# A trunk layer on one Trainium2 core: LayerNorm's sum of squares in a PSUM bank, and one more two-product pair in the up projection

## The chip, the core and the metric

The kernel runs on one core of a Trainium2 chip. The metric is the device time of one execution in microseconds (us); lower is better. The core has five engines with queues of their own, which run beside each other and meet through semaphores: TensorE (PE, the matrix products, with weight loads shown apart as PEld), VectorE (DVE), ScalarE (ACT), GpSimd (POOL) and SyncE (SP, which issues most transfers). Products land in PSUM, which has eight banks of 128 x 512 numbers; everything else lies in SBUF.

## The reference

One decoder layer over 512 tokens of 1024 channels in float32, cut here to what the change touches:

```python
u = rmsnorm(h);  proj = u @ w_in                       # GLU | q | k | v | r | low | gates A, B
c = causal_dwconv(a * sigmoid(g), width 31)            # branch A
c = silu(layernorm(c));  y_conv = c @ w_conv_out       # mean and variance over the channels
y_gla = gla(q, k, v, ...) * silu(r) @ w_gla_out        # branch B, four heads
h = h + (sigmoid(gate_a) * y_conv + sigmoid(gate_b) * y_gla) @ w_o
u2 = rmsnorm(h)
z = causal_dwconv(u2 @ w_ffn_up, width 3)              # 1024 -> 2 x 2816
h = h + (silu(z[:, :2816]) * z[:, 2816:]) @ w_ffn_down
out = rmsnorm(h)
```

## The kernel before, in words

**Products in three parts.** Each float32 operand is split into a high part (`whi` for weights) and the rest (`wlo`); a product is then three: high x low, low x high, high x high (`mm3`, lines 516 to 522). These three lines are nearly all of TensorE's work. A weight tile is 128 rows of 1024 numbers (512 KB); SyncE fetches it into `raw` (four buffers), and `split_weight` (lines 396 to 445) makes its parts in four `whi` and four `wlo` buffers: ScalarE copies the high part, VectorE subtracts it from `raw` for the low part (line 443, or 409 for tiles of other kinds). For the names in `ADDED` (lines 47 and 48) VectorE isn't used: ScalarE writes -`raw` into `wlo` (line 440) and a transfer issued from GpSimd's queue adds the weight tile to it from HBM (line 441). The high part is the same. `LOOK = 2` (line 45): parts are made two tiles ahead.

**Order.** The weights are used in one list, `order`, from line 242 on; each call of `weight` takes the next. A scheduler turns the program into one queue for each engine and picks the buffers, so a change in one stage can move the places of neighbouring instructions in a queue.

**The up projection.** Its 44 tiles of 128 channels come as 22 pairs (i, 22 + i): the value half and the gate half of one block. There are three groups of blocks (`GROUPS`, line 34). The first is ((0, 2), (1, 3), (4, 6), (5, 7)); in each inner pair the first block has the role "first" and the other "second", after the place that it takes in the down projection that follows the group. A plain tile (`col_tile`, line 524) is 8 x 3 products of 512 columns, 24 in all. Two tiles can be had for fewer multiplications (`two_tiles`, line 1313): the tokens are halved, and seven products of weight sums with token sums take the place of eight. That is four weight operands x1, x3, x2, x4 (two, two, two and one steps), each step 4 x 3 products of 256 columns, 84 in all. x3 and x4 are weight sums that GpSimd makes (`two_sums`, lines 377 to 392, line 380 in the profile): three adds of 128 x 512 at x1 and one at x3. VectorE combines the seven results (line 1323). The token sums are made once, by VectorE and ScalarE, in the first group (`ffn_sums`, lines 1276 to 1289 in the profile).

**The plan of a group** (`up_plan`, lines 187 to 231) is a list of steps. In the first group, blocks 0 and 2 are done ahead of it; then blocks 1, 3 and 4 are plain; then come two units. A unit is one two-product pair with a plain block threaded through its parts: pair 6 with block 5, pair 7 with block 8 (a block of the next group). After each block its width-3 convolution runs: ScalarE scales (line 1690), VectorE adds two taps (line 1693), and then the gating and splits for the down projection (`first_gated`, `first_of_pair`, `second_of_pair`, lines 1716 to 1740). The loop at line 1845 carries the plan out; `third` (set when a pair is done) is an order that the next "second" step keeps: it is placed behind the pair's last tap and the third weight sum.

**LayerNorm of branch A** runs beside the merge stage, as a chain of small steps that `fill` (line 496) deals out among the tiles. The mean lies in an "ax" bank of PSUM (there are three). For each of eight channel blocks `ln_center` (line 1002) subtracts the mean (line 1003), squares (line 1005, ScalarE) and adds the square to `stat["sq"]` (line 1009, VectorE). The sum and each square are "btmp" tiles in SBUF, of which there are two. `token_sums` then multiplies the sum with ones.

Of the kernel before, what the change touches and what calls it, by code (L numbers as in the profile page):

```python
# [15 lines left out]
ALU = mybir.AluOpType  # L16
# [5 lines left out]
KT = D // P  # L22
# [6 lines left out]
FT = FF // P  # L29
# [69 lines left out]
def trunk_layer(ctx: ExitStack, tc: tile.TileContext, a: dict, out: bass.AP):  # L99
    nc = tc.nc  # L100
# [33 lines left out]
    def btmp():  # L134
        return tp.tile([P, T], F32, tag="btmp", name=nm("btmp"), bufs=2)
# [50 lines left out]

    def up_plan(gi):


        pairs = GROUPS[gi]  # L190
        whole = range(KT)

        def halves(*cuts):
            return [range(a, b) for a, b in zip((0, *cuts), (*cuts, KT))]

        def unit(q, f, kind):

            a, b = f, FT + f
            x1, x3, x2, x4 = (("part", q, part) for part in ("x1", "x3", "x2", "x4"))
            a1, a2 = (("tile", a, ks) for ks in halves(4))  # L200
            if kind == "opens":
                b1, b2, b3 = (("tile", b, ks) for ks in halves(4, 6))
                seq = [a1, x1, a2, x3, b1, x2, b2, x4, ("second", q), b3]
            elif kind == "closes":
                a1, a2, a3 = (("tile", a, ks) for ks in halves(3, 6))
                seq = [x1, a1, x3, a2, x2, a3, x4, ("second", q), ("tile", b, whole)]
            else:
                a1, a2 = (("tile", a, ks) for ks in halves(5))
                b1, b2 = (("tile", b, ks) for ks in halves(4))
                seq = [x1, a1, x3, a2, x2, b1, x4, ("second", q), b2]  # L210
            return seq + [("first", f)]

        firsts = [p for p, _ in pairs[1:]]
        if gi + 1 < len(GROUPS):
            firsts.append(GROUPS[gi + 1][0][0])
        plan = []
        n = 0
        if gi == 0:
            (p, q), (f, _) = pairs[1:3]
            for i, role in ((p, "first"), (q, "second"), (f, "first")):  # L220
                plan += [("tile", i, whole), ("tile", FT + i, whole), (role, i)]
            n = 2
        while n < len(firsts):
            last = n + 1 == len(firsts) and gi + 1 < len(GROUPS)
            kind = "closes" if last else "opens" if n == 0 else ""
            plan += unit(pairs[n][1], firsts[n], kind)
            n += 1
        if n < len(pairs):
            q = pairs[n][1]
            plan += [("tile", q, whole), ("tile", FT + q, whole), ("second", q)]  # L230
        return plan

    def up_order(plan):
# [767 lines left out]

    def ln_center(k):
        nc.vector.tensor_tensor(conv[k], stat["mean"], conv[k], ALU.add)
        sq = btmp()
        nc.scalar.activation(sq, conv[k], AF.Square)
        if k == 0:
            stat["sq"] = sq
        else:
            nc.vector.tensor_tensor(stat["sq"], stat["sq"], sq, ALU.add)

    def ln_var():
        v = small(NT, "mean")
# [805 lines left out]
    for gi, pairs in enumerate(GROUPS):  # L1818
        acts = []
        if gi == 0:  # L1820

            ws = [weight("w_up", j, 0) for i in pairs[0] for j in (i, FT + i)]
            accs = [mm_bank() for _ in ws]
            for j, lo in [(j, lo) for lo in (0, H) for j in range(3)]:
                late = {(1, 0): (KT - 1, 2), (2, 0): (MID, 3)}.get((j, lo))
                at = {late[0]: lambda t=late[1]: to_channels(normed[t], u2, t)} if late else {}
                col_tile(ws[j], acts2, accs[j], lo, lo + H, at)
            col_tile(ws[3], acts2, accs[3])
            p, q = pairs[0]
# [12 lines left out]
            some_sums()  # L1842
        else:
            found = first_of_pair(w)
        for what, i, *rest in up_plan(gi):
            if what == "tile":
                if 0 in rest[0]:
                    banks[i] = (weight("w_up", i), mm_bank())
                wt, acc = banks[i]
                col_tile(wt, acts2, acc, ks=rest[0])  # L1850
                if KT - 1 in rest[0] and i < FT:
                    values[i] = value(i, acc)
            if what == "part":
                if rest[0] == "x1":
                    units[i] = two_tiles("w_up", i, FT + i, lambda: up_acts, ax_bank)
                done = next(units[i])
                if done:
                    values[i] = value(i, done[0])
                    banks[FT + i] = (None, done[1])
                    third = [taps_at[0], third_ahead()]  # L1860
            if what == "first":
                w = first_gated(i, values.pop(i), banks.pop(FT + i)[1])
                if any(i in pair for pair in pairs):
                    found = first_of_pair(w)
            if what == "second":
                with ExitStack() as order_of:
                    for ins in third:
                        if ins:
                            order_of.enter_context(tc.issue_after(ins.ins))
                    acts.append(second_of_pair(i, values.pop(i), banks.pop(FT + i)[1], w, found))  # L1870
                third = []
            if what in ("first", "second"):
                some_sums()
        if gi < len(GROUPS) - 1:
            seven("w_down", pairs, acts, lambda t, n, c: None)
        else:
            gain3 = load_gain("final_g")
            seven("w_down", pairs, acts, last_complete, last_at, True)
# [90 lines left out]
```

## Time and profile before

| | us |
|---|---|
| median of three runs | 827.72 |
| the three runs | 827.73, 827.72, 824.37 |
| the profiled execution | 824.33 |
| its span, first to last instruction | 822.3 |
| TensorE busy in the span | 808.5 |
| VectorE, ScalarE, GpSimd busy | 707.6, 482.7, 182.4 |
| the first group of the up projection, TensorE | 474.0 to 573.2 |
| LayerNorm's eight centerings, VectorE | 314.9 to 324.1 |

The granted TensorE clock is 0.998 of full speed over the span. A row of a timeline begins with the start and the duration in us and names engine, line, operation, output <- inputs, partitions x elements; what stands in brackets is the engine's idle time before it and who ended it. A row of the groups ends with the busy time in us and the mean duration in ns of one. Matmul durations overlap, so the pace of TensorE is read from the starts.

### The profile page before, as it was taken

What the parts mean: (1) busy time and instruction counts of PE and PEld (TensorE: products, weight loads), DVE (VectorE), ACT (ScalarE), POOL (GpSimd) and SP (SyncE); (2) the same over time, 40 slices, a digit from 0 to 9 for tenths busy, and PEclk for the clock granted to TensorE, in tenths of its full rate; (3) what the DMA queues carried; (4) which work ended last, traced back from release to release, by engine and by line L of the source; (5) the groups of instructions that cost most, each with busy time, mean ns of one, the idle gap of its engine ahead of it and who ended that gap; (6) DMA issues with size and microseconds to landing.
All of it is one profiled execution on the core that took longest, in us unless ns stands there. A gap on an engine that the chain in (4) does not pass through costs nothing.

```text
span 822.3 us, 11449 instructions
## 1 busy us (share of the span) xinstructions
PE 808.5 (98%) x4227; PEld 695.2 (85%) x4227; DVE 707.6 (86%) x1125; ACT 482.7 (59%) x726; POOL 182.4 (22%) x164
## 2 busy tenths in 40 slices
PE   9999999999999999999999999999999999999996
PEld 8888887888887798889988898898889988899885
DVE  6879999999999877595788889979975999789895
ACT  6667788477646574484445546556435663466554
POOL 2016423121203232222001000230133311622012
PEclk9999999999999999999999999999999999999999
DMA  8487886864900433333447623146632447234662
GB/s 325 154 194 166 200 210 168 193 153 103 205 27 26 129 103 103 110 112 111 156 103 219 194 74 103 50 156 163 138 137 83 146 129 166 103 103 173 161 128 102
DMA packets 36759, 114.64 MB, mean 139 GB/s; under 512 B 3720, under 2 KB 8976, under 8 KB 36704
## 3 DMA queue, kind: packets, MB, share of 16 engines
q1 hardware_dynamic: 28912, 86.39, 30.5%
q0 software_dynamic: 7776, 27.53, 19.7%
q8 instruction: 33, 0.54, 0.3%
q14 instruction: 22, 0.18, 0.1%
q10 hardware_dynamic: 16, 0.00, 0.0%
HBM read 111.81 MB, written 2.10 MB: 139 GB/s over the span
## 4 chain that ended last, share of the span: by engine, by line
PE 89%; DVE 4%; issue 3%; DMA 2%; ACT 1%; POOL 0%; POOLq 0%; ACTq 0%; DVEq 0%; SPq 0%
PE mm L520 21%; PE mm L521 21%; PE mm L522 21%; PE cv L520 4%; PE cv L521 4%; PE cv L522 4%; PE ax L522 2%; PE ax L521 2%; PE ax L520 2%; PE mm L734 2%; DVE wlo L409 2%; DMA wlo<-in_w_qk_dram 1%; PE cv L734 1%; PE ax L1201 1%; PE ax L1183 1%
## 5 line engine op out<-in xcount | busy, mean ns | idle before, releaser
L520 PE MATMUL mm<-uh,wlo 128*128 128x512 f32 (+1 forms) x524 | 192.7, 368 | 0.9 <-DMA wlo<-in_w_qk_dram 0.9
L521 PE MATMUL mm<-ul,whi 128*128 128x512 f32 (+1 forms) x524 | 190.7, 364 | 0.0
L522 PE MATMUL mm<-uh,whi 128*128 128x512 f32 (+1 forms) x524 | 190.4, 363 | 0.0
L409 DVE TENSOR_TENSOR wlo<-raw,whi 128x1024 fp32r<-128x1024 f32 x82 | 95.6, 1173 | 30.1 <-ACT whi L408 26.3
L380 POOL TENSOR_TENSOR raw<-raw,raw 128x512 f32<-128x512 f32 x39 | 61.6, 1580 | 240.0 <-DVE wlo L409 122.2
L520 PEld LDWEIGHTS mm<-uh,wlo 128*128 128x128 f32 x524 | 99.0, 189 | 16.7 <-ACT btmp L913 1.3
L522 PEld LDWEIGHTS mm<-uh,whi 128*128 128x128 f32 x524 | 98.8, 189 | 15.7
L521 PEld LDWEIGHTS mm<-ul,whi 128*128 128x128 f32 x524 | 99.0, 189 | 14.7
L408 ACT CAST whi<-raw 128x1024 fp32r<-128x1024 f32 x82 | 79.0, 965 | 38.1 <-PE mm L522 28.5
L438 ACT CAST whi<-raw 128x1024 fp32r<-128x1024 f32 x80 | 83.3, 1046 | 29.1 <-PE mm L522 12.9
L443 DVE TENSOR_TENSOR wlo<-raw,whi 128x1024 fp32r<-128x1024 f32 x50 | 65.9, 1324 | 7.3 <-ACT whi L438 7.1
L408 ACT CAST whi<-kept 128x1024 fp32r<-128x1024 f32 (+1 forms) x40 | 40.1, 1006 | 40.7 <-DVE kept L356 19.2
L880 DVE SCALAR_TENSOR_TENSOR aside<-cv,pp,aside 128x255 f32<-128x255 f32 (+6 forms) x112 | 52.9, 472 | 0.8 <-ACT cv L871 0.8
L409 DVE TENSOR_TENSOR wlo<-kept,whi 128x1024 fp32r<-128x1024 f32 (+1 forms) x40 | 48.2, 1206 | 5.4 <-ACT whi L408 5.2
L880 DVE SCALAR_TENSOR_TENSOR c<-aside,btmp,c 128x249 f32<-128x249 f32 (+14 forms) x103 | 51.4, 509 | 0.7 <-ACT c L876 0.7
L440 ACT ACTIVATE wlo<-raw 128x1024 fp32r<-128x1024 f32 x30 | 31.7, 1058 | 33.8 <-PE mm L520 30.6
L880 DVE SCALAR_TENSOR_TENSOR c<-cv,pp,c 128x255 f32<-128x255 f32 (+14 forms) x103 | 48.6, 472 | 2.9 <-ACT c L876 2.9
L1693 DVE SCALAR_TENSOR_TENSOR tmp<-mm,pp,tmp 128x511 f32<-128x511 f32 (+1 forms) x48 | 35.6, 743 | 4.0 <-ACT tmp L1690 3.9
L1473 DVE TENSOR_TENSOR hres<-hres,mm 128x512 f32<-128x512 f32 (+1 forms) x39 | 25.8, 669 | 3.1 <-PE mm L522 1.7
L1693 DVE SCALAR_TENSOR_TENSOR tmp<-tmp,pp,tmp 128x511 f32<-128x511 f32 (+1 forms) x32 | 27.8, 888 | 0.3
L520 PE MATMUL cv<-uh,wlo 128*128 128x512 f32 (+1 forms) x80 | 27.4, 342 | 0.7 <-DVE tmp L1323 0.7
L1690 ACT ACTIVATE tmp<-mm,pp 128x512 f32<-128x512 f32 x24 | 18.6, 777 | 14.8 <-PE mm L522 14.6
(464 smaller groups left out, 2064.9 us busy)
## 6 DMA issues: line engine op xcount, KB each, us to landing
raw<-in_w_up_dram SPq DMA_DIRECT2D x44, 512.0 KB, 3.6
raw<-in_w_glu_dram SPq DMA_DIRECT2D x16, 512.0 KB, 6.2
raw<-in_w_down_dram SPq DMA_DIRECT2D x15, 512.0 KB, 3.4
wlo<-in_w_glu_dram POOLq DMA_DIRECT2D x12, 512.0 KB, 7.3
kept<-in_w_down_dram POOLq DMA_DIRECT2D x10, 512.0 KB, 5.5
raw<-in_w_v_dram SPq DMA_DIRECT2D x8, 512.0 KB, 6.1
raw<-in_w_qk_dram SPq DMA_DIRECT2D x8, 512.0 KB, 6.6
wlo<-in_w_qk_dram POOLq DMA_DIRECT2D x8, 512.0 KB, 7.1
```

The costliest lines, as they stand in the source:

```text
L380: work = nc.gpsimd.tensor_tensor(out, x, y, ALU.add)
L408: nc.scalar.copy(hi, raw)
L409: two_low[:] = [nc.vector.tensor_tensor(lo, raw, hi.bitcast(F32), ALU.subtract)]
L438: nc.scalar.copy(hi, raw)
L440: pace[0] = nc.scalar.mul(lo, raw, -1.0)
L443: pace[0] = nc.vector.tensor_tensor(lo, raw, hi.bitcast(F32), ALU.subtract)
L520: nc.tensor.matmul(acc, ll, rh, start=first, stop=False, **kw)
L521: nc.tensor.matmul(acc, lh, rl, start=False, stop=False, **kw)
L522: nc.tensor.matmul(acc, lh, rh, start=False, stop=last, **kw)
L880: nc.vector.scalar_tensor_tensor(out[:, j:], x[:, : half_t - j], w, out[:, j:], ALU.mult, ALU.add)
L1473: done = nc.vector.tensor_tensor(hres[t, n][:, c], hres[t, n][:, c], acc[:, c], op)
L1693: nc.vector.scalar_tensor_tensor(z[:, s:], acc[:, : T - s], w[j], z[:, s:], ALU.mult, ALU.add)
```

## The change

It does three things.

- `ln_center`: the sum of squares starts in an "ax" bank (ScalarE writes the first square there), VectorE adds the next six squares onto it in PSUM, and the last add writes the total into a "btmp" tile. One btmp tile less is held over the chain.
- The plans of the groups are written out in `PLANS`. The second and third group's come out as before. In the first group, block 4 (tiles 4 and 26) becomes a two-product pair: blocks 1 and 3 plain, then pair 4 and pair 6 in sequence with block 5 threaded through both, then pair 7 with block 8 as before. The first group has three two-product pairs where it had two. A "first" block can now come from a pair, so the order in `third` is kept there too.
- The low parts of the four plain tiles of blocks 1 and 3 (tiles 1, 23, 3, 25) are put into `ADDED`.

```diff
+PLANS = (
+    (("plain", 1, 3), ("both", 4, 6, 5), ("closes", 7, 8)),
+    (("opens", 10, 9), ("", 11, 20), ("closes", 21, 12)),
+    (("opens", 14, 13), ("", 15, 16), ("", 18, 17), ("plain", 19)),
+)
...
+ADDED |= {("w_up", m) for m in (1, FT + 1, 3, FT + 3)}
...
+        def both(p, q, f):
+
+            x1, x3, x2, x4 = parts(p)
+            y1, y3, y2, y4 = parts(q)
+            (a1, a2), (b1, b2) = cut(f, 4), cut(FT + f, 4)
+            return [x1, a1, x3, a2, x2, x4, role(p), y1, b1, y3, b2, y2, y4, role(q), role(f)]
...
-        sq = btmp()
+        sq = btmp() if k else ax_bank()
         nc.scalar.activation(sq, conv[k], AF.Square)
         if k == 0:
             stat["sq"] = sq
         else:
-            nc.vector.tensor_tensor(stat["sq"], stat["sq"], sq, ALU.add)
+            total = stat["sq"] if k < KT - 1 else btmp()
+            nc.vector.tensor_tensor(total, stat["sq"], sq, ALU.add)
+            stat["sq"] = total
...
             if what == "first":
-                w = first_gated(i, values.pop(i), banks.pop(FT + i)[1])
-                if any(i in pair for pair in pairs):
-                    found = first_of_pair(w)
+                with ExitStack() as order_of:
+                    for ins in third:
+                        if ins:
+                            order_of.enter_context(tc.issue_after(ins.ins))
+                    w = first_gated(i, values.pop(i), banks.pop(FT + i)[1])
+                    if any(i in pair for pair in pairs):
+                        found = first_of_pair(w)
+                third = []
```

In `cut(f, 4)`, `a1` is the first half of block 5's value tile (four of its eight k steps) and `a2` the rest; `b1` and `b2` are the same of its gate tile.

More of the change, by code (lines that the diff above doesn't have):

```diff
@@ L191, in up_plan, with parts, cut @@
         whole = range(KT)
[L193 to L200, printed above, removed]
+        def parts(q):
+            return [("part", q, part) for part in ("x1", "x3", "x2", "x4")]
+        def cut(m, *at):
+            return [("tile", m, range(a, b)) for a, b in zip((0, *at), (*at, KT))]
@@ L201, in unit, with turns, one @@
+        def turns(m, role):
+            return [("tile", m, whole), ("tile", FT + m, whole), (role, m)]
+        def one(q, f, kind):
+            x1, x3, x2, x4 = parts(q)
             if kind == "opens":
-                b1, b2, b3 = (("tile", b, ks) for ks in halves(4, 6))
-                seq = [a1, x1, a2, x3, b1, x2, b2, x4, ("second", q), b3]
+                (a1, a2), (b1, b2, b3) = cut(f, 4), cut(FT + f, 4, 6)
+                seq = [a1, x1, a2, x3, b1, x2, b2, x4, role(q), b3]
             elif kind == "closes":
-                a1, a2, a3 = (("tile", a, ks) for ks in halves(3, 6))
@@ L206, in unit @@
-                seq = [x1, a1, x3, a2, x2, a3, x4, ("second", q), ("tile", b, whole)]
-            else:
[L208 to L215, printed above, removed]
-        plan = []
-        n = 0
@@ L218, in up_plan @@
[L218 to L230, printed above, removed]
+                a1, a2, a3 = cut(f, 3, 6)
@@ new lines, in one @@
+                seq = [x1, a1, x3, a2, x2, a3, x4, role(q), ("tile", FT + f, whole)]
+            else:
+                (a1, a2), (b1, b2) = cut(f, 5), cut(FT + f, 4)
+                seq = [x1, a1, x3, a2, x2, b1, x4, role(q), b2]
+            return seq + [role(f)]
+        def both(p, q, f):
[3 more added lines that the diff above has]
+            return [x1, a1, x3, a2, x2, x4, role(p), y1, b1, y3, b2, y2, y4, role(q), role(f)]
@@ L231, in up_plan, with role @@
+        seconds = {q for _, q in pairs}
+        def role(i):
+            return ("second" if i in seconds else "first", i)
+        plan = []
+        for kind, *units in PLANS[gi]:
+            if kind == "plain":
+                for i in units:
+                    plan += turns(i, role(i)[0])
+            elif kind == "both":
+                plan += both(*units)
+            else:
+                plan += one(*units, kind)
         return plan
```

## The prediction

> **What bounds the kernel now.** I read the page first (span, busy time, chain that ended last), then who waited for whom on TensorE, then the timeline where the two edits lie.
>
> ```profile
> span 822.3 us, 11449 instructions
> ## 1 busy us (share of the span) xinstructions
> PE 808.5 (98%) x4227; PEld 695.2 (85%) x4227; DVE 707.6 (86%) x1125; ACT 482.7 (59%) x726; POOL 182.4 (22%) x164
> ...
> PE 89%; DVE 4%; issue 3%; DMA 2%; ACT 1%; POOL 0%; POOLq 0%; ACTq 0%; DVEq 0%; SPq 0%
> ```
>
> ```profile
> PE mm L520 <- DVE r L1523: 1.9, 1, 1.9
> PE mm L521 <- DVE wlo L409: 1.5, 1, 1.5
> PE mm L640 <- DVE ones L613: 1.1, 1, 1.1
> PE mm L520 <- DMA wlo<-in_w_qk_dram: 0.9, 1, 0.9
> PE cv L520 <- DVE tmp L1323: 0.7, 1, 0.7
> ```
>
> TensorE is busy 98% of the span and is 89% of the chain. Its named waits are single events of 0.7 to 1.9 us. So an edit is worth two things only: the matmul time that it removes, and the part of such a wait that it ends. Work taken off or put on the other engines is worth nothing unless TensorE comes to wait. One wait in the list is touched: the last, 0.7 us on a combine of line 1323.
>
> **Part 1, the extra two-product pair (tiles 4 and 26).** Two plain tiles are 2 x 8 x 3 = 48 products of 512 columns; a pair is 7 steps x 4 x 3 = 84 products of 256 columns. TensorE's timeline gives both rates: first product of the plain tile 26, first of the pair of 6, first after that pair's x1 part.
>
> ```profile
> 525.74 0.39 PE L520 MATMUL cv<-uh,wlo 128*128 128x512 f32 x1
> ...
> 531.18 0.28 PE L520 MATMUL mm<-uh,wlo 128*128 128x256 f32 x1
> ...
> 534.05 0.40 PE L520 MATMUL mm<-uh,wlo 128*128 128x512 f32 x1
> ```
>
> The plain tile takes 531.18 - 525.74 = 5.44 us for 24 products (227 ns each, though each shows 0.39: they overlap). The x1 part takes 2.87 us for 24 (120 ns each). The pair therefore costs 84 x 0.1196 = 10.04 us and replaces 10.88: **-0.84 us**. The column count alone (21504 against 24576) would give -1.36; a short product costs a little over half of a long one. The products lie on the engine that bounds, so nothing hides or eats the gain unless an operand is late.
>
> **Part 2, the sum of squares in PSUM.** VectorE's, GpSimd's and TensorE's timelines around the 0.7 us wait:
>
> ```profile
> 326.03 0.69 DVE L1402 TENSOR_TENSOR h<-mm,h 128x512 f32<-128x512 f32 x1
> 326.64 1.39 DVE L1009 TENSOR_TENSOR btmp<-btmp,btmp 128x512 f32<-128x512 f32 x1
> 327.94 2.31 DVE L409 TENSOR_TENSOR wlo<-raw,whi 128x1024 fp32r<-128x1024 f32 x1
> 330.18 1.77 DVE L1009 TENSOR_TENSOR btmp<-btmp,btmp 128x512 f32<-128x512 f32 x1
> 331.87 0.41 DVE L1323 TENSOR_TENSOR tmp<-tmp,cv 128x256 f32<-128x256 f32 x1
> ```
>
> ```profile
> 326.17 3.00 POOL L380 TENSOR_TENSOR raw<-raw,raw 128x512 f32<-128x512 f32 x2 [13.56 <-ACT btmp L1005]
> 329.13 2.27 POOL L380 TENSOR_TENSOR raw<-raw 128x512 f32<-128x512 f32 x1
> ```
>
> ```profile
> 331.22 0.39 PE L522 MATMUL mm<-oa,whi 128*128 128x512 f32 x1
> 332.34 0.39 PE L520 MATMUL cv<-uh,wlo 128*128 128x256 f32 x1 [0.73 <-DVE tmp L1323]
> ```
>
> ```profile
> L1003 DVE TENSOR_TENSOR c<-ax,c 128x512 f32<-128x512 f32 x8 | 5.1, 684 | 0.0
> ```
>
> While GpSimd adds from 326.17 to 331.4, the VectorE adds that read two SBUF tiles stretch: the sums of squares to 1.39 and 1.77 us, the low part to 2.31. The add with a PSUM input at 326.03 keeps 0.69, and so do the centerings (684 ns). The combine that frees TensorE's bank is behind them in VectorE's queue and begins at 331.87. TensorE should go on 0.23 us after 331.22, at 331.45; it does at 332.34: 0.89 us, and 0.1 more while its pipe refills. In the changed program's queue order the combine stands ahead of the last but one sum of squares and of that low part. The adds and centerings before it all have a PSUM input. From 326.03 I count: one h add 0.6, one centering 0.6, then the combine, ready when its product ends near 327.3. It begins near 327.8, over 3 us ahead of its need. No row shows VectorE *writing* PSUM. Its bounds are the 0.68 of L1003 and the 1.77 of the slowest old sum; I take 0.69, the nearest rows being those with a PSUM input. At 1.77 for each of the five sums ahead of it the combine would begin 5 x 1.08 = 5.4 us later, at 333.2 instead of 331.87 now, and the part would cost 1.3. The last sum goes to SBUF and is needed long after. **-0.95 us**, bounds -1.0 and +1.3.
>
> The Trainium skill, "SBUF — State Buffer", section "Who interferes with whom", says that a VectorE instruction with two SBUF inputs contends with a GpSimd instruction that reads SBUF, and that one with at most one SBUF input, outside the two-port modes, does not. The trace agrees: 1.39 and 1.77 against 0.69 in one stretch. By that rule the new sums can't reach the 1.77, and the part gives -0.95; without it the end of +1.3 has only the distance of the rows against it.
>
> The bank that the sum holds is one of three "ax" banks, and the mean holds another. No other product goes to an ax bank between the mean and the token sums, so nothing queues behind it. The freed btmp buffer lets ScalarE square earlier; ScalarE isn't near the path there.
>
> **Part 3, low parts of tiles 1, 23, 3 and 25 by adding transfers.** VectorE loses four operations of 1.22 us; ScalarE gains four, GpSimd's queue four transfers of 512 KB, all ahead of its adds for pair 4.
>
> ```profile
> L440 ACT ACTIVATE wlo<-raw x30: 1041/1060/1089, 38.5 to 216.9; 128x1024 fp32r<-128x1024 f32 x30
> ```
>
> ```profile
> DMA to landing us min/median/max: 5.3/7.2/10.3
> ```
>
> ```profile
> DMA to landing us min/median/max: 8.5/9.0/9.5
> ```
>
> ```profile
> 498.74 0.78 ACT L1690 ACTIVATE tmp<-mm,pp 128x512 f32<-128x512 f32 x1
> ```
>
> ```profile
> 509.42 0.39 PE L520 MATMUL mm<-uh,wlo 128*128 128x512 f32 x1
> ```
>
> The first landing row is of all 30 such transfers, the second of two issued 1.9 us apart (at 205.3 and 207.2). The tight one is tile 3. In the changed ScalarE queue its -raw copy stands right behind the operation at 498.74, which waits for the product ending there and is delayed to about 499.3 by two earlier copies. So the copy ends near 501.1 and the transfer leaves then. Tile 25's leaves 2 us later. As the first of a close pair I give it 7.2 to 8.5 us: landing at 508.3 to 509.6. Tile 3's first product, which reads the low part, is due at 509.42. **+0.1 us**, bounds 0 and 501.1 + 10.3 - 509.42 = 2.0. The others have room. Tile 1 is due two tiles earlier, 509.42 - 2 x 5.44 = 498.5. Its buffer's last reader ends one tile and two halves before that (5.4 + 2 x 2.9), at 487.2; the copy ends at 488.3 and the transfer lands by 496.8. Tiles 23 and 25 have 2 us or more. ScalarE's four copies fall in idle stretches (it is busy 4.5 to 5.8 of each 10 us below).
>
> **Does VectorE keep up with two pairs back to back?** The windows 500 to 530, one low part and one slowed add, GpSimd's adds for a pair, and one combine:
>
> ```profile
> 500.00:510.00 10.00, 10.00 (x46) 8.29 (x45) 10.00 (x15) 4.45 (x7) 0.00 (x0) 1.00 0.50 158
> 510.00:520.00 10.00, 10.00 (x46) 8.29 (x45) 9.80 (x13) 5.78 (x8) 0.00 (x0) 1.00 0.00 0
> 520.00:530.00 10.00, 10.00 (x46) 8.29 (x45) 10.00 (x13) 4.70 (x6) 4.62 (x3) 1.00 0.17 54
> ```
>
> ```profile
> 524.57 1.77 DVE L1707 TENSOR_TENSOR f<-tmp,tmp 128x512 f32<-128x512 f32 x1
> ...
> 528.67 1.22 DVE L409 TENSOR_TENSOR wlo<-raw,whi 128x1024 fp32r<-128x1024 f32 x1
> ```
>
> ```profile
> 521.09 3.01 POOL L380 TENSOR_TENSOR raw<-raw,raw 128x512 f32<-128x512 f32 x2 [42.22 <-DVE wlo L443]
> ```
>
> ```profile
> L1323 DVE TENSOR_TENSOR tmp<-tmp,ax 128x256 f32<-128x256 f32 x8 | 3.3, 412 | 2.8 <-PE ax L522 2.8
> ```
>
> Behind the length of the stretch stand the busy times of TensorE, its weight loads, VectorE, ScalarE and GpSimd. VectorE is full, and x1 of pair 6 was ready at 529.9 for a need at 531.18: 1.3 us of room. The pair adds 3.5 low parts for 2 and three combines, 1.5 x 1.22 + 3 x 0.41 = 3.1 us, and 1.5 to 2.5 us of slowing by GpSimd's adds (the 1.77 above is one of them); the transfers take 4.9 us away: about even. But what is removed stands ahead of pair 4 and what is added stands behind its x1. Going down the changed VectorE queue with these durations, and with products due at 5.44 us a tile and 2.87 a part from 509.42 on, x1 of pair 4 is ready at 514 (due 520.3), x3 at 522 (525.9), x1 of pair 6 at 532 (535.8; its buffer comes free at 528.8), x3 at 537 (541.5), x3 of pair 7 at 552.5 (556.3). The least room is 3.8 us. **0**, bounds 0 and +2. The order of the rest (w_down, last group) is as now, 0.8 us earlier.
>
> **Sum.** -0.84 - 0.95 + 0.1 = -1.7 us. Span 822.3 to 820.6; the profiled execution's 824.33 to 822.6. The runs shown are 824.37, 827.72 and 827.73: the profiled one is at the lower end, the median 3.4 us above it, and the trace of one execution can't say what that spread is. On the median the forecast is 827.72 - 1.7 = **826.0 us**.
>
> **The rivals.**
> - *The wait moves* (one gain only). The combine is in time, but TensorE then waits for the low part behind it, still slowed to 2.3 us. For: it is two SBUF inputs beside GpSimd. Against: from the quoted 331.22 on come 12 products of the pair, 12 long ones of another tile, and only then its first, 4 us after the 331 at which it would end. Gives -0.75 us: 823.6, on the median 827.0.
> - *A late transfer* (slower). Tile 3's low part lands last and takes the place of the wait removed. It decides when landing takes over 8.3 us, and cancels both gains at 10.1. The row's 10.3 gives 2.0 - 1.8 = +0.2; if tile 1's pair is late by as much (10.3 ends at 498.6 for 498.54), +0.3: 824.6, on the median 828.0. For: the 8.5 to 9.5 of two that lie close, and the one transfer wait in TensorE's list. Against: the transfer engines are light there (share 0.50 in 500 to 510, 0.00 after). The Trainium skill, same page and section, speaks for it: a transfer issued by GpSimd can starve for descriptors while VectorE runs in a two-port mode. No row here separates such a wait from the 5.3 to 10.3; VectorE's operations in that stretch are mostly two-input ones, of which the page infers that they do not do this, so I leave the chance at 0.15.
> - *VectorE falls behind between pairs 4 and 6.* Its room of 3.8 us is used up if GpSimd's adds slow it by more than 6 us; a loss of 2 us then nets +0.2: 824.5 and 827.9. Against: the transfers free it first.
> - *The pair doesn't save.* Weight loads are 8.3 us of each 10 with long products; were short ones bound by loads, 0 instead of -0.84: 823.5 and 826.9. Against: the 120 ns row is itself of such products.
>
> **How the numbers follow.** Forecast 0.62; the wait moves 0.13; late transfer 0.15; VectorE behind 0.07; no saving 0.03. All of these lie within 4 us, and 0.5% is 4.1 us, about what a measurement of this kernel can tell from no change. So "faster" needs the runs to fall on the lower end where before's fell on the upper (822.6 against 827.7), which I give 0.24; "slower" needs several of the bounds at once, or the reverse spread: 0.09. Range: from the lower level with all gains and no late transfer, 824.33 - 1.8 less 1.2 for an execution that scatters lower, 821.3, to the upper level with the worst transfer, 827.73 + 1.3 = 829.0.
>
> **What would show it.** The two products of 512 and 256 columns at 227 and 120 ns; 84 of the short kind in pair 4; no wait of TensorE on line 1323's combine near 331; sums of squares at 0.69 us beside GpSimd; a wait of TensorE on wlo<-in_w_up of under 0.5 us near 509. A wait there of 1 us or more, or a wait on line 409's low part between 520 and 545, would make me wrong.

## The result, and the profile after

The changed kernel takes **829.63 us** (median of 15 runs, 827.95 to 831.21); the kernel before, run as often on the same chip, 825.88 (824.11 to 827.73). The ratio is 1.0048, 95% interval 1.0037 to 1.0058: it is **slower by 4.0 us** by that ratio (the medians differ by 3.75), where 1.7 us faster was forecast. The time lies 0.6 us above the range. The 15 runs of before also show that the two levels of its first three runs were scatter.

The profiled execution takes 828.43 us (before 824.33). Its page: the span, the busy times, and the shares of the chain that ended last.

```profile
span 826.4 us, 11556 instructions
## 1 busy us (share of the span) xinstructions
PE 810.0 (98%) x4263; PEld 698.1 (84%) x4263; DVE 711.2 (86%) x1126; ACT 488.6 (59%) x736; POOL 188.1 (23%) x172
...
PE 83%; DVE 9%; ACT 5%; issue 2%; DMA 1%; POOL 0%; POOLq 0%; SPq 0%; DVEq 0%; ACTq 0%
```

TensorE's share of the chain fell from 89% to 83%; VectorE and ScalarE took it. In the changed code lines are 11 to 13 later: the products are 531 to 533, `two_tiles`' copies of a product (`put`) 1333 and its combines 1336, the low part of a pair's weights 420, GpSimd's adds 391, the high part in `fsplit` 1725, the adds of `second_of_pair` 1746 to 1748. Each of a pair's seven products is named after its token operand: x1 has a11 and a12, x3 has n2 and s1, x2 has n3 and s4, x4 has a22. `f` is a second block's gated product, `w` a first block's with a difference behind it; `v` holds three more differences and sums of the two, and all are operands of the down projection. TensorE's waits, longest first (total us, times, longest):

```profile
PE ax L531 <- ACT tmp L1333: 1.9, 1, 1.9
...
PE mm L531 <- DVE tmp L1336: 0.8, 1, 0.8
PE mm L531 <- ACT tmp L1333: 0.7, 1, 0.7
```

Three waits are new, all on operations of `two_tiles`; the 0.7 on a combine near 331 is gone. The same product's start in both traces shows where the time lies:

| TensorE at (before), us | after minus before, us |
|---|---|
| 7 | -0.25 |
| 146 | -0.85 (wait for a q/k transfer 0.3 instead of 0.9) |
| 289 | -1.26 (wait for r 1.4 instead of 1.9) |
| 332 | -2.15 (LayerNorm's wait gone) |
| 560, behind the pairs | +3.78 |

The steps at 146 and 289 lie outside of the change and vary from run to run. What was lost lies between 518 and 561 us, but for 0.3 us of the span behind the last product. TensorE's timeline there, at the two waits in pair 4 (the first product of the s4 part, and the first of x4):

```profile
530.59 0.28 PE L533 MATMUL mm<-btmpq,whi 128*128 128x256 f32 x1
...
532.72 0.39 PE L531 MATMUL ax<-gainq,wlo 128*128 128x256 f32 x1 [1.85 <-ACT tmp L1333]
...
534.67 0.41 PE L533 MATMUL ax<-gainq,whi 128*128 128x256 f32 x1
535.92 0.58 PE L531 MATMUL mm<-uh,wlo 128*128 128x256 f32 x1 [0.83 <-DVE tmp L1336]
```

From start to start, less the 0.12 us of a product, 2.0 us and 1.1 us are lost, 0.25 more behind the second, and 0.85 in pair 7 near 560: 4.2 us. The rows at 534.67 show a second loss: the short products now take 0.41 instead of 0.28. The windows of the stretch (length, then busy times of TensorE, weight loads, VectorE, ScalarE, GpSimd; then TensorE's granted clock, the transfer engines' share, GB/s):

```profile
528.00:532.00 4.00, 2.87 (x19) 2.43 (x17) 3.50 (x4) 0.50 (x2) 3.92 (x3) 1.00 0.27 111
532.00:536.00 4.00, 2.45 (x13) 2.16 (x13) 3.39 (x5) 3.23 (x5) 0.65 (x1) 0.68 0.00 0
536.00:540.00 4.00, 4.00 (x19) 4.00 (x20) 3.21 (x4) 2.68 (x4) 0.48 (x1) 0.50 0.33 95
540.00:544.00 4.00, 4.00 (x27) 3.70 (x27) 3.77 (x5) 2.83 (x6) 0.81 (x1) 0.97 0.66 186
```

Behind the first wait the clock falls to half. 26 products go at 0.21 us instead of 0.12: 2.3 us. So in this execution, from 332 to 560: -0.8 for the pair, +4.2 of waits, +2.3 of clock, together +5.7, and 3.78 + 2.15 = 5.9 was read (0.1 us of refill behind a wait makes the rest).

**Why TensorE waits.** GpSimd's, VectorE's and ScalarE's timelines at that place:

```profile
527.97 3.28 POOL L391 TENSOR_TENSOR raw<-raw,raw 128x512 f32<-128x512 f32 x2 [3.50 <-DMA raw<-in_w_up_dram]
531.21 1.45 POOL L391 TENSOR_TENSOR raw<-raw 128x512 f32<-128x512 f32 x1
```

```profile
528.60 1.50 DVE L1747 TENSOR_TENSOR v<-v,w 128x256 f32<-128x256 f32 x1
530.14 1.39 DVE L1748 TENSOR_TENSOR v<-f,v 128x256 f32<-128x256 f32 x1
532.43 1.04 DVE L1726 TENSOR_TENSOR sl<-v,sh 128x768 fp32r<-128x768 f32 x1 [0.90 <-ACT sh L1725]
533.65 1.23 DVE L420 TENSOR_TENSOR wlo<-raw,whi 128x1024 fp32r<-128x1024 f32 x1 [0.18 <-ACT whi L419]
534.79 0.74 DVE L1706 SCALAR_TENSOR_TENSOR tmp<-cv,pp,tmp 128x511 f32<-128x511 f32 x1
535.45 0.41 DVE L1336 TENSOR_TENSOR tmp<-tmp,mm 128x256 f32<-128x256 f32 x1
```

```profile
531.56 0.83 ACT L1725 CAST sh<-v 128x768 fp32r<-128x768 f32 x1 [3.50 <-DVE v L1748]
532.30 0.36 ACT L1333 COPY tmp<-ax 128x256 f32<-128x256 f32 x1
532.56 1.05 ACT L419 CAST whi<-raw 128x1024 fp32r<-128x1024 f32 x1
```

Read it from the bottom. TensorE's s4 products, due at 530.7, wait for the copy at 532.30. What it copies (the s1 part) ended near 526.7. The copy stands in ScalarE's queue behind the split of block 3's `v`, and ScalarE sat idle for 3.5 us until VectorE's last `v` add. That add and the one before it, two SBUF inputs each, take 1.50 and 1.39 us while GpSimd makes the weight sums for pair 6; an add of this shape takes 0.41 elsewhere (508.91 in the same trace). Then VectorE waits in turn for the split and for the high part that stands behind ScalarE's copy, and the combine of 535.45, for which x4 waits, comes last.

The theory from this (**A**): GpSimd's adds for the next pair and the places of these few instructions in two queues make the loss; two pairs back to back bring them together. Rivals: **B**, the four transfers; **C**, the adds that write PSUM; **D**, the pair saves nothing; **E**, the copy's place alone; **F**, VectorE's total amount of work, in whatever order.

### The profile page after: what moved, and what is told of

The parts are those of the page before. It is cut to its first block, busy times and chain, and to the rows that moved or that the text cites. A ratio compares the mean times of both kernels' runs of the same rounds, so it can differ in the third digit from the quotient of the medians.

```text
span 826.4 us, 11556 instructions
## 1 busy us (share of the span) xinstructions
PE 810.0 (98%) x4263; PEld 698.1 (84%) x4263; DVE 711.2 (86%) x1126; ACT 488.6 (59%) x736; POOL 188.1 (23%) x172
## 4 chain that ended last, share of the span: by engine, by line
PE 83%; DVE 9%; ACT 5%; issue 2%; DMA 1%; POOL 0%; POOLq 0%; SPq 0%; DVEq 0%; ACTq 0%
PE mm L531 20%; PE mm L532 20%; PE mm L533 20%; PE cv L531 3%; PE cv L533 3%; PE cv L532 3%; DVE wlo L420 2%; PE ax L533 2%; PE ax L532 2%; PE ax L531 2%; PE mm L745 2%; DVE tmp L1706 1%; DVE kept L1289 1%; PE cv L745 1%; PE ax L1214 1%
## 5 line engine op out<-in xcount | busy, mean ns | idle before, releaser
L531 PE MATMUL mm<-uh,wlo 128*128 128x512 f32 (+1 forms) x508 | 185.0, 364 | 1.1 <-DVE tmp L1336 0.8
L532 PE MATMUL mm<-ul,whi 128*128 128x512 f32 (+1 forms) x508 | 182.7, 360 | 0.0
L533 PE MATMUL mm<-uh,whi 128*128 128x512 f32 (+1 forms) x508 | 182.4, 359 | 0.0
L531 PEld LDWEIGHTS mm<-uh,wlo 128*128 128x128 f32 x508 | 97.0, 191 | 15.9 <-DVE tmp L1336 1.1
L533 PEld LDWEIGHTS mm<-uh,whi 128*128 128x128 f32 x508 | 96.8, 191 | 14.0
L451 ACT ACTIVATE wlo<-raw 128x1024 fp32r<-128x1024 f32 x34 | 35.8, 1057 | 36.4 <-PE mm L531 33.0
L1333 ACT COPY tmp<-mm 128x256 f32<-128x256 f32 x38 | 14.0, 368 | 32.9 <-PE mm L533 32.4
L531 PE MATMUL cv<-uh,wlo 128*128 128x512 f32 (+1 forms) x88 | 32.2, 365 | 0.0
L532 PE MATMUL cv<-ul,whi 128*128 128x512 f32 (+1 forms) x88 | 31.8, 361 | 0.0
L533 PE MATMUL cv<-uh,whi 128*128 128x512 f32 (+1 forms) x88 | 31.8, 361 | 0.0
```

The costliest lines, as they stand in the source:

```text
L451: pace[0] = nc.scalar.mul(lo, raw, -1.0)
L531: nc.tensor.matmul(acc, ll, rh, start=first, stop=False, **kw)
L532: nc.tensor.matmul(acc, lh, rl, start=False, stop=False, **kw)
L533: nc.tensor.matmul(acc, lh, rh, start=False, stop=last, **kw)
```

## The experiments

All ratios are to the kernel before on the same chip, with 95% intervals.

**1. The LayerNorm edit alone** on the kernel before.

```diff
-        sq = btmp()
+        sq = btmp() if k else ax_bank()
...
```

> The kernel before with the LayerNorm edit alone (the sum of squares in a PSUM bank). Theory A (the loss is made between 530 and 541 us, where pair 4 and pair 6 lie back to back: ScalarE's copy of a product, and VectorE's combine, stand behind the split of block 3's v tile, whose adds GpSimd's adds have slowed; TensorE waits 1.9 and 0.8 us and its clock then falls to half for 7.5 us): 0.9 us faster than before, a ratio of 0.999, no wait of TensorE on line 1323's combine near 331. Rival C (the adds that write PSUM cost something that the trace of the whole change hides): 1 us or more slower, ratio 1.001 or above. Both keep the clock near 0.998.

Measured: 823.76 us against 824.98; ratio 0.9978 (0.9965 to 0.9990). C is out: the edit gains, and no wait is left at 331. The forecast 0.9989 lies inside the interval. Of all kernels here this one is the fastest against before.

**2. Block 4 plain again, the rest kept.**

```diff
-    (("plain", 1, 3), ("both", 4, 6, 5), ("closes", 7, 8)),
+    (("plain", 1, 3, 4), ("", 6, 5), ("closes", 7, 8)),
```

> The changed kernel with block 4 as two plain tiles again: the LayerNorm edit and the four low parts by transfers stay. Theory A: everything that was lost lay in pair 4 and behind it, so the time is that of before less the 0.9 us of LayerNorm, ratio 0.998 to 1.000, no wait on line 1333's copies and no stretch of half clock. Rival B (the transfers that add low parts cost the time, as late landings or as contention): still 2 us or more above before, ratio 1.002 or above.

Measured: 824.93 against 824.98; ratio 0.9995 (0.9983 to 1.0007). The loss came with the pair. But a new wait of TensorE stands in this trace, 0.8 us at tile 3's first product, 9.0 us after its transfer left (502.59 to 511.62; the landing is at 511.48). The profile names a VectorE operation as what ended it; the product starts 0.13 to 0.14 us after the landing here and in experiments 9 and 12, so it is read as a wait for the transfer. Experiment 12 takes that up.

**3. One exchange in ScalarE's queue**: the copy ahead of the split of `v`.

```diff
-        y = fsplit(v, 3 * H, "s")
...
+            if what == "rest":           # a step of the plan, behind x3 of pair 4
+                with tc.issue_after(puts[-1].ins):
+                    rests.pop()()       # the split of v
```

> The changed kernel with one pair of ScalarE's instructions exchanged: the copy of pair 4's s1 product stands ahead of the split of v, not behind it; every other queue is unchanged. If the place of the copy in ScalarE's queue is the cause by itself (rival E), the 1.9 us wait goes, and with it the half clock: 5 us faster than the changed kernel, ratio to before 0.998. Theory A in its full form says that VectorE is as late as ScalarE: the combine that began at 535.45 stays where it is, behind the split's low part, so the first wait of 1.9 us goes and the second grows from 0.8 to about 2.7 us; the sum is the same and the ratio stays at 1.003 to 1.006, with the clock falling behind that one wait.

Measured: 831.24 against 824.98; ratio 1.0062 (1.0045 to 1.0080). TensorE's timeline has one wait where there were two:

```profile
534.43 0.28 PE L533 MATMUL ax<-gainq,whi 128*128 128x256 f32 x1
538.09 0.58 PE L531 MATMUL mm<-uh,wlo 128*128 128x256 f32 x1 [3.38 <-DVE tmp L1336]
```

E is out: the copy in time helps nothing while VectorE's combine is late. From start to start 3.5 us are lost, where it was 2.0 and 1.1, and the clock falls with the one wait too (at 537.0).

**4. The slowed adds and the split behind pair 4's first combine.** All of `v`'s last two adds and its split are placed so, in both queues.

```diff
...
+                with tc.issue_after(combines[-2].ins):
+                    rests.pop()()      # v's n2, s4, high and low part
```

> The changed kernel with the two v adds that GpSimd slowed (1.50 and 1.39 us) and the split of v moved behind pair 4's first combine, in VectorE's and ScalarE's queues; nothing is left out. Theory A: the copy and the combine are in time, the waits of 1.9 and 0.8 us go, the clock stays at 1.00 through 530 to 541, and the whole change gains what its parts promised: 1.5 to 2 us below before, ratio 0.998 (0.999 if the wait of 0.7 us near 560 stays). Rivals B and D (transfers cost, or the pair saves nothing): the time stays above before, ratio 1.001 or more, though the waits are gone.

Measured: 828.49 against 824.98; ratio 1.0041 (1.0024 to 1.0057). Half right. Pair 4 has no wait left. Pair 6, 15 us on, has the same two:

```profile
549.08 0.38 PE L531 MATMUL ax<-gainq,wlo 128*128 128x256 f32 x1 [0.95 <-ACT tmp L1333]
552.76 0.39 PE L531 MATMUL mm<-uh,wlo 128*128 128x256 f32 x1 [1.99 <-DVE tmp L1336]
```

There block 4's gating product and its difference (lines 1721 and 1737) take 1.59 and 1.40 us beside GpSimd's adds for pair 7, and the copy stands behind their split. In the changed kernel these adds were as slow, but TensorE came to pair 6 later.

**5. The same at pair 6 as well.**

```diff
-        gated(i, za, acc, w[:, :T])
...
+            zb = ffn_conv(acc, FT + i)
+            rests.append(...)          # w's product, difference and split, behind pair 6's first combine
...
```

> As the run before with v's adds and split behind pair 4's first combine, and block 4's gating product, difference and split (the w adds of 1.59 and 1.40 us, beside GpSimd's adds for pair 7, and the split that ScalarE's copy waited for at 548.14) moved behind pair 6's first combine in the same way; nothing is left out. Theory A says that each pair that follows a pair directly has the same collision, and that nothing else costs: the waits of 0.9 and 2.0 us near 548 and 550 go, the clock holds, 1.5 to 2 us below before, ratio 0.998. Rival F (VectorE's total work is what is late, whatever its order): the wait only moves on, to pair 7 or to a low part, with 1 to 3 us, and the ratio stays above 1.002.

Measured: 825.62 against 824.81; ratio 1.0009 (0.9998 to 1.0020). On the same chip the changed kernel had 1.0067 (experiment 8): the order gives back 4.8 us. Neither side's number came out. The two waits are gone and the clock is 0.998, but pair 7 now waits 1.4 us for a copy behind an activation that waits for VectorE's taps, and the gain of 1.8 does not show.

**6. GpSimd's adds held back** until the `v` and `w` adds are done.

```diff
+            if p in held:
...
+                add(o, held[p], held[p])   # one column, reads v (pair 6) or w (pair 7)
             add(three[:, left], one[:, left], two[:, left])
...
```

> The changed kernel with GpSimd's adds for pair 6 held until block 3's last v add is done, and those for pair 7 until block 4's w difference is done (a one-column add on GpSimd that reads them stands ahead); VectorE's and ScalarE's queues are unchanged. If GpSimd's adds are what made the v adds late (theory A), the two v adds take 0.41 us instead of 1.50 and 1.39, the split runs near 530 instead of 531.6, the 1.9 us wait goes, and what is left is a combine behind a low part slowed to some 2 us: waits of 0.5 to 1.5 us in pair 4 and no or a shorter stretch of half clock, 2 to 5 us below the changed kernel, ratio 0.999 to 1.003. If VectorE is late for its own work alone (rival F), the waits stay at 2.5 us or more and the ratio at 1.004 to 1.006.

Measured: 830.41 against 824.81; ratio 1.0060 (1.0046 to 1.0075). VectorE's timeline:

```profile
531.95 0.42 DVE L1753 TENSOR_TENSOR v<-v,w 128x256 f32<-128x256 f32 x1
532.40 0.42 DVE L1754 TENSOR_TENSOR v<-f,v 128x256 f32<-128x256 f32 x1
533.73 1.43 DVE L1730 TENSOR_TENSOR sl<-v,sh 128x768 fp32r<-128x768 f32 x1 [0.90 <-ACT sh L1729]
535.08 2.30 DVE L424 TENSOR_TENSOR wlo<-raw,whi 128x1024 fp32r<-128x1024 f32 x1
...
537.97 0.40 DVE L1340 TENSOR_TENSOR tmp<-tmp,mm 128x256 f32<-128x256 f32 x1
```

One half of A is shown: the adds fall to 0.42, and the wait for the copy is gone. Its number is wrong: begun 1.7 us later (6.5 us behind the x3 add ahead of them instead of 4.8), GpSimd's adds slow what comes next, the low parts `sl` and `wlo`, and the combine is as late. TensorE waits 2.6 us for it, and 1.8 in pair 6. To shift the adds by so little isn't enough; the low parts that they now hit stand ahead of the same combine.

**7. The wait filled.** Eight products that nobody reads are put into the first wait, in the unused half of a bank.

```diff
...
+            for k in range(8):
+                nc.tensor.matmul(z[:, H:], w[0][:, k * P : (k + 1) * P], ...)
```

> The changed kernel with eight products of 256 columns that nobody reads put between pair 4's n3 and s4 products, into the unused half of a PSUM bank: TensorE works about 1 us of the 1.9 us wait away with them. The wait's end is set by ScalarE, so they cost nothing there. If the half clock is the result of the wait's length (theory A: 3.3 us of the loss), TensorE's idle time falls to under 1 us and the clock stays at 1.00 from 530 to 541: 3 us below the changed kernel, ratio 1.001. If the clock fell for another reason (the stretch, the operands), the half clock stays, and the ratio at 1.004 to 1.006.

Measured: 829.29 against 824.81; ratio 1.0063 (1.0045 to 1.0082). The windows behind the wait:

```profile
532.00:536.00 4.00, 3.09 (x25) 2.78 (x23) 2.94 (x3) 2.75 (x5) 2.35 (x2) 1.00 0.00 0
536.00:540.00 4.00, 2.50 (x21) 2.40 (x21) 3.77 (x7) 2.61 (x4) 0.00 (x0) 1.00 0.00 0
```

The clock holds, so its fall was the result of the wait's length. The time doesn't follow: experiment 8 has 1.0067 on the same chip, and no difference can be told. TensorE comes to pair 6 earlier and waits there, 1.4 us for a combine, which it did not in the changed kernel. While TensorE was slow VectorE caught up; the 2.3 us were hardly a cost that comes on top. The record of the changed kernel's 15 runs fits: the five with a mean granted clock of 0.997 to 0.999 have a median of 829.3, the eight with 0.994 one of 830.1, all well above 825.88.

**8. The changed kernel again.**

> The changed kernel itself, on the chip that runs the three others: ratio 1.004 to 1.006, the waits of 1.9 and 0.8 us and the stretch of half clock behind them, as a second profile of them.

Measured: 830.11 against 824.81; ratio 1.0067 (1.0050 to 1.0084). The profile has the waits on the same two operations (2.9 and 1.0 us) and half clock behind the first.

**9. Without GpSimd's weight sums** for pairs 4, 6 and 7; the first raw tile stands in for the sums. VectorE's and ScalarE's queues stay.

```diff
-            three = raw_tile()
+            three = one if name == "w_up" and p in (4, 6, 7) else raw_tile()
+            if three is one:
+                return
...
```

> The changed kernel without GpSimd's weight sums for pairs 4, 6 and 7 (twelve adds left out; x3 and x4 are then the first raw tile itself, so the up projection's numbers are not the reference's). VectorE's and ScalarE's queues are as in the changed kernel. In the changed kernel's trace the adds lengthen VectorE's operations between 523 and 560 us by 0.7 + 1.1 + 1.0 + 0.4 + 0.9 + 1.0 + 0.7 = 5.8 us. If this contention is what makes VectorE late (theory A), no wait over 0.5 us is left in pairs 4, 6 and 7: 5 to 7 us below the changed kernel, ratio 0.998 to 0.9995. If VectorE's own work is too much at this place (rival F), waits of 1.5 us or more stay and the ratio is above 1.002.

Measured: 824.62 against 824.98; ratio 0.9993 (0.9985 to 1.0002). VectorE's timeline, in the same order as the changed kernel's rows above:

```profile
526.91 0.43 DVE L1751 TENSOR_TENSOR v<-v,w 128x256 f32<-128x256 f32 x1
527.37 0.43 DVE L1752 TENSOR_TENSOR v<-f,v 128x256 f32<-128x256 f32 x1
529.08 0.96 DVE L1730 TENSOR_TENSOR sl<-v,sh 128x768 fp32r<-128x768 f32 x1 [1.29 <-ACT sh L1729]
530.74 1.23 DVE L424 TENSOR_TENSOR wlo<-raw,whi 128x1024 fp32r<-128x1024 f32 x1 [0.70 <-ACT whi L423]
...
533.61 0.41 DVE L1340 TENSOR_TENSOR tmp<-tmp,mm 128x256 f32<-128x256 f32 x1
```

No wait over 0.5 us is left in the three pairs, and VectorE even idles. This is the run that decides: same queues, same work on VectorE, and the loss is gone. F in its plain form is out. The edit does two more things: the splits of x3 and x4 no longer wait for GpSimd, and a `raw` buffer stays free. The chain read above begins at neither: VectorE has no idle time ahead of the two slow adds, and they are slow while GpSimd runs. The time is not yet the promised gain, since a wait for a transfer has appeared ahead of the pairs:

```profile
PE mm L535 <- DMA wlo<-in_w_up_dram: 1.0, 1, 1.0
```

Forecast gains of 0.95 and 0.84 less that 1.0 make -0.8 us, 0.9990, inside the interval.

**10. Less work on VectorE**: three low parts of blocks 3 and 4 left out. This also changed one place in ScalarE's queue: another copy of pair 4 (of the n2 product) fell behind the split.

```diff
...
+        if (gi, block_at[0]) in ((0, 3), (0, 4)):
+            return lambda c, n=1: (hi[:, c * H : (c + n) * H],) * 2
...
```

> The changed kernel without the low parts of the down projection's operands from blocks 3 and 4 (three subtractions on VectorE of 0.68, 1.04 and 1.02 us left out; the high part stands in for the low part, so the output isn't the reference's). GpSimd's adds stay. If VectorE's amount of work is the cause (rival F), 2.5 us less work gives back about as much: 2 to 3 us below the changed kernel, ratio 1.002 to 1.003. If the order is (theory A: the slowed v adds and the split stand ahead of the copy and the combine), the v adds are as late as ever, the copy's wait of 1.9 us or more stays, only the combine comes 1 us earlier: ratio 1.003 to 1.006.

Measured: 828.19 against 824.98; ratio 1.0036 (1.0023 to 1.0048). TensorE waits 2.7 us for a copy behind the split, now one part earlier. 2.7 us less work beside the same slowed adds leaves most of the loss. Because of the extra exchange the run doesn't say how much of the work's amount counts.

**11. Half a tile ahead of pair 7**, on top of experiment 5.

```diff
-    (("plain", 1, 3), ("both", 4, 6, 5), ("closes", 7, 8)),
+    (("plain", 1, 3), ("both", 4, 6, 5), ("opens", 7, 8)),
```

> As the run with both splits moved, and half a tile of block 8 placed ahead of pair 7's first part instead of behind it (the sequence that the second group's first unit has). Nothing is left out. Theory A: pair 7's wait of 1.6 us for a ScalarE copy that stands behind an activation waiting for VectorE's taps goes, as TensorE comes to it 2.7 us later; the change then gives what its parts promise, ratio 0.998 to 0.9995, better than both kernels. Rival F: the wait only moves to the tile of block 8 or to the down projection's start, ratio 1.000 to 1.002.

Measured: 826.19 against 824.98; ratio 1.0018 (1.0006 to 1.0030). Pair 7's wait is gone, others stand in its place: 1.0 us on a combine in pair 6, 0.8 and 0.7 in the down projection. What F said of the next place came true, and its ratio too. That VectorE has no room to give in this stretch while GpSimd's adds run beside it is a reading of this; no run here tests it by itself.

**12. The four transfers alone** on the kernel before.

```diff
+ADDED |= {("w_up", m) for m in (1, FT + 1, 3, FT + 3)}
```

> The kernel before with the four low parts by transfers alone. The sum of the prediction has 0 to +0.1 us for it. With the LayerNorm edit beside it a wait of 0.8 us was seen near 510, where tile 3 is due. Theory A (the transfers aren't the loss, but the late landing of the prediction is real when the copy leaves late): ratio 1.000 to 1.0015, a wait of up to 1 us near 510. Rival B (the transfers cost more): ratio 1.003 or more.

Measured: 825.73 against 824.98; ratio 1.0009 (1.0001 to 1.0018). The wait is there, 0.9 us near 510. So B is out as the cause, and the late transfer of the prediction's rival is real, but only in experiments 2, 9 and 12, where GpSimd makes no sums at that place and a weight load runs beside the transfer (last section).

**13. The changed kernel without the transfers.**

```diff
-ADDED |= {("w_up", m) for m in (1, FT + 1, 3, FT + 3)}
```

> The changed kernel without the four transfers: VectorE subtracts the low parts of tiles 1, 23, 3 and 25 again (4 x 1.22 = 4.9 us ahead of pair 4). If the transfers gave VectorE room that it lacks behind them (the prediction's step: the transfers free it first), the waits of pair 4 grow by up to 4.9 us: ratio 1.006 to 1.011. If the order and GpSimd's adds decide by themselves and VectorE has that room anyway, the ratio stays at 1.004 to 1.007.

Measured: 830.27 against 824.96; ratio 1.0064 (1.0050 to 1.0079). The changed kernel had 1.0048 and 1.0067: no difference can be told. 4.9 us of VectorE's work ahead of pair 4 moved the wait (here 2.8 us on a combine in pair 6) and not its size.

## Why the prediction was wrong

- **The baseline: too high.** The 826.0 stood on a median of three runs; 15 runs put it at 825.88, and the same sum from there gives 824.2, so the miss is 5.4 us. The interval is also 0.9 us to either side, where 4.1 us was taken for what a measurement can tell.
- **The pair's pace: right.** x1 of pair 4 is 24 products from 518.05 to 520.93, 120 ns each; pair 4 has 84 (so D is out). Experiment 9, without the waits, has the time that the two gains less the transfer wait give.
- **LayerNorm: right.** The wait of 0.9 us is gone. The sums that write PSUM keep 0.69 us beside GpSimd, and the combine is early:

```profile
326.20 0.42 DVE L1336 TENSOR_TENSOR tmp<-tmp,cv 128x256 f32<-128x256 f32 x1
326.54 0.69 DVE L1021 TENSOR_TENSOR ax<-ax,btmp 128x512 f32<-128x512 f32 x1
327.14 1.58 DVE L420 TENSOR_TENSOR wlo<-raw,whi 128x1024 fp32r<-128x1024 f32 x1
```

  The rule quoted from the Trainium skill ("SBUF — State Buffer", "Who interferes with whom") fits: at 326.54 one SBUF input and 0.69; at 327.14 two and 1.58 instead of 1.22.
- **The transfers: right here, by luck of the neighbours.** The copy and the landing came as the working has them (7.1 us from issue to landing). No wait for one in the changed kernel; a wait of about 1.0 us in experiments 2, 9 and 12, which the bound of 2.0 covers. What the working doesn't have is the weight load that runs beside the transfer in these three.
- **"Does VectorE keep up with two pairs back to back?", taken as 0 with bounds 0 and +2: this step failed.** In the profiled execution it measured 4.2 us of waits and 2.3 of half clock. Three things were wrong in it. First, the walk down VectorE's queue gave a due time only to weights ("the least room is 3.8 us"). These were in time: TensorE waits for no low part in the pairs. What came late were the two operations that free TensorE's banks, a ScalarE copy and a VectorE combine. The copy had 4.0 us (526.7 to 530.7, half a tile and the n3 products), the combine 1.4 us (the s4 products: in the new sequence x4 follows x2 with no tile between); and both stand behind another block's work in strict order. Second, GpSimd's slowing was a lump of 1.5 to 2.5 us in the balance. At its place it makes 0.41 into 1.4 to 1.5 twice, with a split on ScalarE, the copy and TensorE in a row behind it. Third, the same rule that the LayerNorm part relied on was not applied to single operations here: the `v` and `w` adds have two SBUF inputs, and GpSimd's adds for the next pair run just then.
- **The rival "VectorE falls behind between pairs 4 and 6"** had the right place, a chance of 0.07 and a price of 2 us, with the condition that GpSimd's adds slow VectorE by more than 6 us. The slowing between 523 and 560 us adds up to 5.8 us; the waits began well before that was spent, at the first two adds.
- **What would make me wrong** named a wait on line 409's low part. The waits were on the copy and the combine of the same pair.

Settled: without GpSimd's adds the loss is gone (9), the order of two queues decides where and how much TensorE waits (3, 4, 5, 11), transfers and LayerNorm aren't it (1, 2, 12, 13). Open: a complete kernel with the third pair that is faster than before was not found. Moving the weight sums off GpSimd, which experiment 9 points to, was not tried in a complete form.

## What to carry to other kernels

When a step adds work to a busy engine, give a due time to each operation that another engine waits for, above all the short ones that free a PSUM bank, and look at what stands ahead of it in its own queue and what that waits for. An engine's slowing by a neighbour is entered at the instruction that it hits and followed through the queues behind it, not as a sum over the stretch. And a loss of clock behind a wait isn't a cost by itself while the engine that was waited for is still late.

## What was not expected of the hardware

- **Half clock behind a short wait.** In the 15 profiles (20 to 790 us of each span; a wait is the time from start to start less the product's pace), 13 waits of TensorE from 2.0 to 3.5 us begin at full clock; with 8 of them the granted clock fell to 0.50, from 2.4 to 4.0 us after the wait began, for 3.4 or 6.8 us. Of some 45 waits from 1.0 to under 2.0 us none did so by itself. The shortest with a fall is the 2.0 at 530.59 above; one of 2.9 (experiment 10) had none, with 1.00 in the windows around it:

```profile
532.00:536.00 4.00, 2.13 (x17) 2.13 (x18) 1.61 (x2) 3.28 (x6) 1.80 (x2) 1.00 0.00 0
```

  The Trainium skill, "TensorE: Matmul & The Clock Gate", "Part 1: The HAM clock gate", has half rate after at least one idle window of about 3.4 us, in windows that run freely. The traces agree on free windows: between 20 and 790 us the clock changes only at whole multiples of 3.41 us from its first rise to full speed. They don't agree on the length. With TensorE's waits added up within each window at full clock, the eight windows with 2.1 us or more are the ones behind which the clock fell, and none with 1.9 us or less is followed by half clock. So the 2.0 us at 530.59, all in the window from 530.03 to 533.44, were enough, and the 2.9 of experiment 10 were not, split by a boundary into 1.6 and 1.3; the measurement decides. The scatter of before, which the prediction left open, goes in part with the clock: of its 29 runs beside experiments 9 to 12 the six with a granted clock of 0.996 took 826.05 to 827.15 us, the others, at 0.997 to 0.999, 823.88 to 826.01. The traces of experiments 1, 2 and 6 show one such stretch near 139 us, behind the wait for a q/k transfer.
- **A VectorE operation that begins during a GpSimd add stands until the add is nearly done, short or long.** VectorE operations with two SBUF inputs went from 0.41 to 1.39 and 1.50, from 0.68 to 1.59 and from 1.22 to 2.30: +1.0, +1.1, +0.9, +1.1. So the short ones suffer most, three to four times their length. The traces show where the like sizes come from. In the 15 profiles (20 to 790 us), 611 such operations of 256 to 1024 columns began while a GpSimd add ran. 570 of them took longer by what was left of that add less 0.13 us (to within 0.06 us), which is 1.14 us at most. The other 41 weren't slowed at all; some of these began within 0.1 us of the add, as the one at 528.00 in the changed kernel (0.68). Of 210 that already ran when an add began, 201 weren't slowed. So it matters which of the two begins first, and the slowing can be counted from the add's end at the operation that it hits.
- **The same transfer, 6.3 to 9.1 us.** Tile 3's low part landed 8.9 to 9.1 us after its issue in experiments 2, 9 and 12, and 6.3 to 8.2 us in the nine other profiles that have this transfer (7.1 in the changed kernel's). In those three GpSimd adds nothing in this stretch, and SyncE issues a weight load of 512 KB 1.5 us behind the transfer; it lands 0.2 to 0.4 us after it. In the nine GpSimd makes pair 4's sums, for which a third tile takes one of the four `raw` buffers, and no load is issued between the transfer's issue and its landing. So the shorter landing goes with a missing load as much as with the adds; which of the two decides was not tried by itself.
